# Turning the last gated chunk earlier, and placing two of the merge's sums later, in a decoder layer

## The chip, the cores and the metric

The kernel runs on one core of a Trainium2 chip. The metric is the device time of one execution in microseconds. The times before are 371.0, 371.18 and 372.96 us, median 371.18 us.

## The reference

One decoder layer on 256 tokens of width 1024, all in float32: a pooling mixer and causal attention side by side, a cross-attention into 256 memory tokens, and a SwiGLU feed-forward of inner width 2816. Each of the three parts is added to 2^(1/4) times the residual and normalized. Only the last part matters here:

```
def swiglu(h, w_gate, w_up, w_down):
    return (jax.nn.silu(h @ w_gate) * (h @ w_up)) @ w_down

h = layer_norm(DEEPNORM_ALPHA * h + swiglu(h, w_gate[l], w_up[l], w_down[l]), ln3_g[l], ln3_b[l])
```

## The kernel before

**Precision.** Every product of float32 matrices is made of three fast products: each operand is split into a high half (a cast on ScalarE, `nc.scalar.copy`) and a low half (value minus high half, `nc.vector.tensor_sub` on VectorE), and high x high, high x low and low x high are summed in PSUM. In the profile `w137h` and `w137l` are the halves of weight tile 137, `w132r` a raw weight tile as it was loaded. Weights are loaded and split on the fly (class `Stream`): `ws.get` splits some tiles ahead of use and, where a raw buffer becomes free, issues the next load on SyncE's queue (SP, L122).

**The feed-forward.** The inner width is cut into 11 chunks (`NFC`) of 256 columns. For chunk c the loop (`for c in range(1, NFC)`, L1032) makes the gate and up products in two PSUM banks (`pg`), one per half of the tokens; `gated(c, t, ps)` (L942, L943) applies silu on ScalarE and multiplies on VectorE, giving `sg`. The down products need the gated chunk with its columns on the partitions. So the chunk is turned: `gated_out(c)` transposes its 32x32 blocks on VectorE (L435, `gs`) and writes it to DRAM from SP (L438, `gd`); `gated_in(c)` reads it back with four transfers that put the blocks in their places (L446, `gr`); `gated_split(c)` splits it into `gTh` (L414, ScalarE) and `gTl` (L415, VectorE). For chunks 0 to 9 these steps are spread over the loop's next passes; for chunk 10, the last, they are listed by hand after the loop.

**The down product.** The output has four pieces, upper left C11, upper right C12, lower left C21 and lower right C22: two halves of the tokens by two halves of the columns. The inner chunks 0 to 8 use seven products instead of eight (a Strassen-like scheme): sums of weight blocks and of token blocks go into four shared PSUM banks p1, p5, p6, p7 (`x` in the profile) inside the loop, and the remaining products (`four`, `fourth`) into the accumulators `acc`. Chunks 9 and 10 (`c_dn`, weight tiles 135 to 138) are multiplied plainly, piece by piece, C11, C12, C21, and C22 in two parts of 256 columns (L1150 to L1152). `down()` is a generator that yields after each product. A hand-written table, `events`, says ahead of which of its first 23 steps another piece of work is issued on the other engines.

**The merge.** `merge()` is a second generator, for VectorE. With u1 = p1, u2 = u1 + p6 (L1104) and u3 = u2 + p7 (L1113), it makes r[n] = ALPHA * h + u for the four pieces (`onto`, L1100): r[0] from u1, r[1] from u2 plus p5 (L1110), r[2] from u3, r[3] from u3 plus p5 (L1119). For C12 and C21 r is added into the accumulator, before their products of chunks 9 and 10 (`seed`, L1068): the first of these products overwrites nothing and has to wait for the seed. For C11 r and the finished accumulator are added afterwards (L1174). C22 is seeded (two operations of 256 columns) after its first products (L1157). Statistics (L715), centring and scaling follow piece by piece, and the rows are stored.

**Order.** Each engine works through its own instructions in the order in which the program issues them, and waits for others by semaphores; transfers issued on SP leave in SP's order.

Of the kernel before, what the change touches and what calls it, by code (L numbers as in the profile page):

```python
# [24 lines left out]
NFC = DFF // CW  # L25
# [10 lines left out]
SEVEN, LAG, LATE = 9, 2, 4  # L36
# [6 lines left out]
class Stream:  # L43
# [118 lines left out]
    def next(self):  # L162

        i = len(self.tiles)
        return i + (2 if i < len(self.items) and self.items[i][0] == "sums" else 1)
# [28 lines left out]
def decoder_layer(  # L194
# [21 lines left out]
    def accbank(name):  # L216
        return pa.tile([P, 512], F32, tag="acc", name=name)
# [157 lines left out]
    def proj_n(pss, numbers, yT, last=True):  # L375

        for k in range(KD):
            for t, ps in pss.items():
                three(ps, pair(yT, ALL, k, slice(t * P, (t + 1) * P)), ws.get(numbers, k), k == 0, k == KD - 1)
            if last:  # L380
                ws.done(numbers, k)
            yield
# [22 lines left out]
    def run(gen, n=None):  # L405

        while n is None or n > 0:
            if next(gen, gen) is gen:
                return False
            n = None if n is None else n - 1  # L410
        return True

    def split(h, l, ps):
        nc.scalar.copy(h, ps)  # L414
        nc.vector.tensor_sub(l, ps, r32(h))  # L415
# [14 lines left out]
    def turned(blocks, n, name, queue=nc.sync):  # L430

        st = sp.tile([P, 4, n, 32], F32, name=f"{name}s", tag="pair", bufs=3)
        for at, src in blocks:
            m = src.shape[1]
            nc.vector.transpose(st[:, :, at:at + m, :].rearrange("p j m b -> p m j b"),  # L435
                                src.rearrange("p m (j b) -> p m j b", b=32))
        via = hp.tile([P, 4, n * 32], F32, name=f"{name}d")
        queue.dma_start(via, st.rearrange("p j m b -> p j (m b)"))  # L438
        return via

    def landed(via, n, name, queue=nc.sync, raw=None):

        if raw is None:
            raw = sp.tile([P, 4, n, 32], F32, name=f"{name}r", tag="pair", bufs=3)
        for j in range(4):
            queue.dma_start(raw[32 * j:32 * (j + 1)].rearrange("p i m b -> p i (m b)"),  # L446
                              via[:, j, :].rearrange("(i a) r -> a i r", i=4))
        return raw
# [245 lines left out]
    class Norm:  # L694
# [15 lines left out]
        def measure(self, c0, c1):  # L710
            self.take(self.r[:, c0:c1])
# [55 lines left out]
    def until(gen):  # L767

        for got in gen:
            if got is not None:  # L770
                return got
# [167 lines left out]
    def gated(c, t, ps):  # L939

        sg = sgs[c][:, :, t, :]
        nc.scalar.activation(sg, ps[:, :CW].rearrange("p (f b) -> p f b", f=2), AF.Silu, bias=0.0, scale=1.0)  # L942
        nc.vector.tensor_mul(sg, sg, ps[:, CW:].rearrange("p (f b) -> p f b", f=2))  # L943
# [3 lines left out]
    def gated_out(c):  # L947
        via[c] = turned([(0, sgs[c].rearrange("p f t b -> p (f t) b"))], 4, "g")

    def gated_in(c):  # L950
        via[c] = landed(via[c], 4, "g")
# [3 lines left out]
    def token_sums(c):  # L955
        raw = via[c]
        s_raw[c] = sp.tile([P, 4, 4, 32], F32, name="sraw", tag="pr", bufs=PR_BUFS)
        if c == 0:
            s_raw["fourth"] = nmp.tile([P, KD, P], F32, name="S4", tag="S")
        a11, a21, a12, a22 = [raw[:, :, m, :] for m in range(4)]  # L960
        s1, s2, s3 = [s_raw[c][:, :, m, :] for m in range(3)]
        nc.gpsimd.tensor_add(s1, a21, a22)  # L962
        nc.gpsimd.tensor_sub(s2, s1, a11)  # L963
        nc.gpsimd.tensor_sub(s3, a11, a21)  # L964
        own = s_raw[c][:, :, 3, :]
        s4_raw = own if c == SEVEN - 1 else s_raw["fourth"][:, c].rearrange("p (i b) -> p i b", i=4)
        nc.gpsimd.tensor_sub(s4_raw, a12, s2)

    def token_sums_split(c):
        hl = [sp.tile([P, 4, P], F32R, name=f"S{n}", tag="pr", bufs=PR_BUFS) for n in range(2)]  # L970
        sums_of[c] = [(hl[0][:, m], hl[1][:, m]) for m in range(3)]
        n = 3
        if c == SEVEN - 1:
            s4[c], n = (hl[0][:, 3], hl[1][:, 3]), 4
        split(*[s[:, :n].rearrange("p m (i b) -> p i m b", i=4) for s in hl], s_raw[c][:, :, :n])

    def fourth_split(c0, c1):
        hl = [sp.tile([P, 4, P], F32R, name=f"S4{n}", tag="pr", bufs=PR_BUFS) for n in range(2)]
        for c in range(c0, c1):
            s4[c] = hl[0][:, c - c0], hl[1][:, c - c0]  # L980
        split(*[s[:, :c1 - c0] for s in hl], s_raw["fourth"][:, c0:c1])

    def gated_split(c):
        i, f = divmod(2 * c, KD)
        h, l = [g[:, f:f + 2, :].rearrange("p f (t i b) -> p (f t) i b", t=T, i=4) for g in gT[i]]
        split(h, l, via[c].rearrange("p i m b -> p m i b"))
# [15 lines left out]
    def shared_products(c):  # L1002

        if not shared:
            shared.extend(bank("x") for _ in range(4))
        p1, p5, p6, p7 = shared
        s1, s2, s3 = sums_of[c]
        for numbers, ops in zip(c_sums[c], (((p1, gblock(c, 0, 0), 0), (p6, s2, 512)), ((p5, s1, 0), (p7, s3, 512)))):
            for ps, y, c0 in ops:
                product(ps, y, numbers, c0, c == SEVEN - 1)  # L1010
            ws.done(numbers, 0)
# [14 lines left out]
    def by_row():  # L1026

        for gen in gu1:
            while run(gen, 2):
                yield  # L1030

    for c in range(1, NFC):  # L1032
        sgs.append(sp.tile([P, 2, T, P], F32, name="sg", tag="pr", bufs=PR_BUFS))
        pss = {t: second[t] if c == 1 else accbank("pg") for t in range(T)}
        gu = by_row() if c == 1 else proj_n(pss, c_gu[c], h2T)
        run(gu, 1)
        gated_out(c - 1)
        run(gu, 2)
        if c > 1:
            gated_split(c - 2)  # L1040
            if c - 2 < SEVEN:
                token_sums(c - 2)
        run(gu, 2)
        gated_in(c - 1)
        run(gu, 1)
        if 0 <= c - 2 < SEVEN:
            token_sums_split(c - 2)
        if c == NFC - 1:
            fourth_split(0, 4)
        run(gu)  # L1050
        for t in range(T):
            gated(c, t, pss[t])
        if 0 <= c - LAG < SEVEN:
            shared_products(c - LAG)

# [32 lines left out]
    def merge():  # L1088

        p1, p5, p6, p7 = shared  # L1090
        for t in range(T):
            norms.append(Norm(3, h2[:, t, :]))
        r = [norms[t].r[:, h * 512:(h + 1) * 512] for t in range(T) for h in range(2)]
        tok = [h2[:, t, h * 512:(h + 1) * 512] for t in range(T) for h in range(2)]

        def u(i):
            return sp.tile([P, 512], F32, name=f"u{i}", tag="pr", bufs=PR_BUFS)

        def onto(n, u):
            nc.vector.scalar_tensor_tensor(r[n], tok[n], ALPHA, u, op0=OP.mult, op1=OP.add)  # L1100

        u1, u2 = u(1), u(2)
        nc.scalar.copy(u1, p1)
        nc.vector.tensor_add(u2, u1, p6)  # L1104
        yield
        onto(0, u1)
        yield
        onto(1, u2)
        yield
        nc.vector.tensor_add(r[1], r[1], p5)  # L1110
        yield
        u3 = u(3)
        nc.vector.tensor_add(u3, u2, p7)  # L1113
        yield
        onto(2, u3)
        yield
        onto(3, u3)
        yield
        nc.vector.tensor_add(r[3], r[3], p5)  # L1119
        yield  # L1120

    def down():

# [16 lines left out]
        for piece in (*PIECES[:3], (1, 512, LAST), (1, LAST, D)):  # L1140
# [18 lines left out]
            yield piece  # L1159

    dn, parts = down(), merge()
    events = {
        2: lambda: gated_out(NFC - 1), 4: lambda: fourth_split(4, SEVEN - 1), 6: lambda: gated_split(NFC - 2),
        7: lambda: gated_in(NFC - 1), 18: lambda: gated_split(NFC - 1),
    }
    events.update({step: lambda: run(parts, 1) for step in (8, 9, 11, 13, 14, 16, 17, 19)})
    for step in range(23):
        events.get(step, lambda: None)()
        run(dn, 1)

    until(dn)
    norm = norms[0]
    for c in (0, 256):
        nc.vector.tensor_add(norm.r[:, c:c + 256], norm.r[:, c:c + 256], acc[PIECES[0]][:, c:c + 256])  # L1174
        norm.measure(c, c + 256)

    def measure(norm, ps):
        for c in range(0, ps.shape[1], 256):
# [89 lines left out]
```

## Time and profile before

| | us |
|---|---|
| profiled execution, device time | 370.71 |
| its span, first to last instruction | 368.9 |
| TensorE (PE) busy | 360.5 |
| weight loads of TensorE (PEld) busy | 311.3 |
| VectorE (DVE) busy | 312.1 |
| ScalarE (ACT) busy | 197.3 |
| GpSimd (POOL) busy | 68.9 |
| median of the three runs | 371.18 |

All times are in us from the start of the span. In a row of a timeline stand the start, the duration, the engine, the line, the operation, what it writes and reads, and in brackets the engine's idle time before it with what ended it. Rows of one engine can overlap a little, because an operation starts while the one ahead drains; what an operation costs its queue is the distance to the next start. A matmul's end is modelled, so for TensorE too the starts are what counts.

### The profile page before, as it was taken

Reading aid. Unit: us, or ns where it says so; the run is one execution under the profiler, and the core shown is the slowest. Engines: PE = TensorE matmul, PEld = TensorE weight load, DVE = VectorE, ACT = ScalarE, POOL = GpSimd, SP = SyncE. Lnnn points to the kernel's source line nnn. Section 1 sums busy time; section 2 is a strip of 40 time slices with the busy share of each in tenths; the row PEclk is TensorE's granted clock in tenths of the full one; section 3 lists DMA queues with packets and bytes.
Section 4 is the critical chain, followed back from the end, with each engine's and each line's share of the span. In section 5 each row is a group of like instructions: output and inputs, shape, how many; then the busy total and the mean of one; then the engine's idle time right before and its main releaser. Section 6 shows DMA issues by size and latency. Waiting matters only on the chain.

```text
span 368.9 us, 5709 instructions
## 1 busy us (share of the span) xinstructions
PE 360.5 (98%) x1995; PEld 311.3 (84%) x1995; DVE 312.1 (85%) x462; ACT 197.3 (53%) x298; POOL 68.9 (19%) x102
## 2 busy tenths in 40 slices
PE   9999999999999999999999999999999999999893
PEld 9997998997888899988888888888888888888682
DVE  5778899994699788765879989999998999789974
ACT  5666865753153665564127636754764664579101
POOL 1000058140010003220010024315402422400000
PEclk9999999999999999999999999999999999999998
DMA  7997699699525995944105988779769877656311
GB/s 246 416 421 297 207 318 327 247 253 396 211 89 167 370 372 203 329 148 151 57 2 198 344 287 285 289 245 346 266 224 338 274 270 262 225 170 195 117 49 65
DMA packets 33836, 89.24 MB, mean 242 GB/s; under 512 B 4240, under 2 KB 12304, under 8 KB 33680
## 3 DMA queue, kind: packets, MB, share of 16 engines
q1 hardware_dynamic: 31520, 83.77, 64.0%
q0 software_dynamic: 1712, 4.72, 4.0%
q10 hardware_dynamic: 576, 0.39, 0.3%
q8 instruction: 15, 0.25, 0.3%
q14 instruction: 13, 0.11, 0.1%
HBM read 81.53 MB, written 7.34 MB: 241 GB/s over the span
## 4 chain that ended last, share of the span: by engine, by line
PE 93%; DVE 4%; issue 1%; ACT 0%; DVEq 0%
PE pg L352 11%; PE pg L351 11%; PE pg L353 11%; PE pxk L369 6%; PE pxq L369 6%; PE pqk L487 6%; PE acc L351 4%; PE acc L352 4%; PE acc L353 4%; PE pu L369 3%; PE x L352 2%; PE x L351 2%; PE x L353 2%; PE xv L352 2%; PE xv L351 2%; PE xv L353 2%
## 5 line engine op out<-in xcount | busy, mean ns | idle before, releaser
L962 POOL TENSOR_TENSOR sraw<-gr 128x128 f32<-128x128 f32 x9 | 9.8, 1094 | 94.7 <-DMA gr<-gd 87.8
L724 POOL TENSOR_TENSOR rs<-mv,mhalf 128x1 f32<-128x1 f32 x6 | 4.4, 735 | 100.2 <-DVE mv L722 100.2
L438 POOL DMA_DIRECT2D pd<-ps x4 | 2.4, 612 | 48.4 <-DVE ps L435 48.1
L524 ACT ACTIVATE pr<-pr,mx 128x128 f32<-128x128 f32 (+1 forms) x16 | 7.1, 444 | 8.2 <-DVE mx L555 8.2
L963 POOL TENSOR_TENSOR sraw<-sraw,gr 128x128 f32<-128x128 f32 x9 | 10.7, 1192 | 0.7
L1204 ACT COPY r<-acc 128x512 f32<-128x512 f32 (+1 forms) x2 | 1.0, 480 | 17.2 <-DVE st L715 17.1
L414 ACT CAST h2Th<-tp 128x512 fp32r<-128x512 f32 x4 | 2.4, 588 | 14.6 <-PE tp L425 14.6
L446 POOL DMA_DIRECT2D pt<-pd x16 | 8.8, 555 | 6.6 <-ACT w23h L144 3.7
L942 ACT ACTIVATE sg<-pg 128x256 f32<-128x256 f32 x22 | 7.9, 381 | 3.2 <-PE pg L353 3.1
L964 POOL TENSOR_TENSOR sraw<-gr 128x128 f32<-128x128 f32 x9 | 9.1, 1009 | 0.0
L943 DVE TENSOR_TENSOR sg<-sg,pg 128x256 f32<-128x256 f32 x22 | 8.4, 415 | 0.4 <-ACT sg L942 0.3
L446 POOL DMA_DIRECT2D xr<-xd x12 | 6.6, 560 | 8.5 <-DMA xd<-xs 5.3
L414 ACT CAST gTh<-gr 128x512 fp32r<-128x512 f32 x11 | 6.8, 614 | 2.6 <-DMA gr<-gd 2.6
L415 DVE TENSOR_TENSOR gTl<-gr,gTh 128x512 fp32r<-128x512 f32 x11 | 7.8, 708 | 0.4 <-ACT gTh L414 0.4
L438 POOL DMA_DIRECT2D xd<-xs x3 | 1.7, 576 | 34.0 <-DVE xs L435 34.0
L435 DVE STREAM_TRANSPOSE gs<-sg 128x512 f32<-128x512 f32 x11 | 7.7, 701 | 0.0
L729 DVE SCALAR_TENSOR_TENSOR r<-r,mv,g 128x512 f32<-128x512 f32 (+1 forms) x10 | 7.5, 781 | 0.2
L524 ACT ACTIVATE xpr<-xs,mx 128x256 f32<-128x256 f32 x8 | 3.7, 470 | 7.0 <-DVE mx L535 7.0
L414 ACT CAST S<-sraw 128x384 fp32r<-128x384 f32 (+1 forms) x9 | 4.7, 523 | 4.6 <-POOL sraw L964 4.6
L715 DVE BATCH_NORM_STATS2 st<-r 128x6 f32<-128x512 f32 (+1 forms) x10 | 6.4, 641 | 0.3
L529 DVE RECIPROCAL sm<-sm 128x2 f32<-128x2 f32 x12 | 2.0, 164 | 5.5 <-ACT xpr L524 4.4
L531 DVE TENSOR_SCALAR pr<-pr,sm 128x128 f32<-128x128 f32 (+1 forms) x16 | 6.1, 422 | 0.3
(1389 smaller groups left out, 1501.0 us busy)
## 6 DMA issues: line engine op xcount, KB each, us to landing
gd<-gs SPq DMA_DIRECT2D x11, 256.0 KB, 5.5
gr<-gd SPq DMA_DIRECT2D x44, 64.0 KB, 2.0
pd<-ps POOLq DMA_DIRECT2D x4, 384.0 KB, 4.2
pt<-pd POOLq DMA_DIRECT2D x16, 96.0 KB, 7.3
g<-in_ln_g SPq DMA_DIRECT2D x3, 512.0 KB, 4.4
b<-in_ln_b SPq DMA_DIRECT2D x3, 512.0 KB, 6.1
wr<-in_w_qkv SPq DMA_DIRECT2D x5, 256.0 KB, 4.8
mr<-in_mem_t SPq DMA_DIRECT2D x1, 1024.0 KB, 12.0
```

The costliest lines, as they stand in the source:

```text
L351: nc.tensor.matmul(ps, wa, ya, start=start, stop=False, skip_group_check=part)
L352: nc.tensor.matmul(ps, wa, yb, start=False, stop=False, skip_group_check=part)
L353: nc.tensor.matmul(ps, wb, ya, start=False, stop=stop, skip_group_check=part)
L369: nc.tensor.matmul(pss[f], w[:, s], y, start=k == 0 and f == 0 and n == 0, stop=k == KD - 1 and n == 2, skip_group_check=True)
L414: nc.scalar.copy(h, ps)
L446: queue.dma_start(raw[32 * j:32 * (j + 1)].rearrange("p i m b -> p i (m b)"), via[:, j, :].rearrange("(i a) r -> a i r", i=4))
L487: nc.tensor.matmul(qk[i][:, f, :], w[:, c * P:(c + 1) * P], y, start=k == 0 and f == 0 and w is hi and y is x_hi, stop=k == KD - 1 and w i ...
L524: nc.scalar.activation(dst[:, j, :], src[:, j, :], AF.Exp, bias=mx[:, j:j + 1], scale=sign, accum_out=sm[:, j:j + 1])
L943: nc.vector.tensor_mul(sg, sg, ps[:, CW:].rearrange("p (f b) -> p f b", f=2))
L962: nc.gpsimd.tensor_add(s1, a21, a22)
L963: nc.gpsimd.tensor_sub(s2, s1, a11)
L964: nc.gpsimd.tensor_sub(s3, a11, a21)
```

## The change

Two things move. No operation is added, dropped or resized.

First, the last gated chunk (chunk 10). Its turn and its write to DRAM are issued right behind its gating product inside the loop, instead of at step 2 of the down product; its read back at step 5 instead of 7; its split at step 12 instead of 18.

Second, the merge. Of its sums, onto 0 (upper left) is issued behind the two seeds, when the products of C11 have been issued; onto 3 and its p5 sum (lower right) behind C11's sums and statistics. What stays at the table's steps are u1 and u2 (8), onto 1 (9), its p5 (11), u3 (16) and onto 2 (17).

```diff
@@ the loop over chunks
         for t in range(T):
             gated(c, t, pss[t])
+        if c == NFC - 1:
+            gated_out(c)
         if 0 <= c - LAG < SEVEN:
             shared_products(c - LAG)
@@ merge()
         nc.vector.tensor_add(u2, u1, p6)
-        yield
-        onto(0, u1)
         yield
         onto(1, u2)
         yield
@@
         onto(2, u3)
         yield
+        onto(0, u1)
+        yield
         onto(3, u3)
-        yield
         nc.vector.tensor_add(r[3], r[3], p5)
-        yield
@@ after down()
     events = {
-        2: lambda: gated_out(NFC - 1), 4: lambda: fourth_split(4, SEVEN - 1), 6: lambda: gated_split(NFC - 2),
-        7: lambda: gated_in(NFC - 1), 18: lambda: gated_split(NFC - 1),
+        4: lambda: fourth_split(4, SEVEN - 1), 5: lambda: gated_in(NFC - 1), 6: lambda: gated_split(NFC - 2),
+        12: lambda: gated_split(NFC - 1),
     }
-    events.update({step: lambda: run(parts, 1) for step in (8, 9, 11, 13, 14, 16, 17, 19)})
+    events.update({step: lambda: run(parts, 1) for step in (8, 9, 11, 16, 17)})
     for step in range(23):
         events.get(step, lambda: None)()
         run(dn, 1)

     until(dn)
+    run(parts, 1)
     norm = norms[0]
     for c in (0, 256):
         nc.vector.tensor_add(norm.r[:, c:c + 256], norm.r[:, c:c + 256], acc[PIECES[0]][:, c:c + 256])
         norm.measure(c, c + 256)
+    run(parts)
```

On VectorE, at the end of the chunk loop (`sg` is the gated chunk 10, `gs` its turned blocks, `w127l` and so on the low halves of weight tiles):

```order
 L943 TENSOR_TENSOR sg<-sg,pg 128x2x128 x2
+L435 STREAM_TRANSPOSE gs<-sg 128x4x4x32
 L145 TENSOR_TENSOR w127l<-w124r,w127h 128x1024
 L145 TENSOR_TENSOR w128l<-w125r,w128h 128x1024
 L145 TENSOR_TENSOR w129l<-w126r,w129h 128x1024
 L145 TENSOR_TENSOR w130l<-w127r,w130h 128x1024
-L435 STREAM_TRANSPOSE gs<-sg 128x4x4x32
 L158 TENSOR_TENSOR w131l<-t_2847,w131h 128x1024
```

The turn stands ahead of four weight splits that it stood behind.

On VectorE from the merge to the last p5 sum, before (`u_3603`, `u_3604`, `u_3640` are u1, u2, u3; `gTl` is the low half of chunk 10; the two seeds follow the last row):

```order
L1100 SCALAR_TENSOR_TENSOR r<-h_1881,u_3603 128x512
L158 TENSOR_TENSOR w134l<-t_3106,w134h 128x1024
L1100 SCALAR_TENSOR_TENSOR r<-h_1881,u_3604 128x512
L145 TENSOR_TENSOR w135l<-w130r,w135h 128x1024
L1110 TENSOR_TENSOR r<-r,x 128x512
L145 TENSOR_TENSOR w136l<-w131r,w136h 128x1024
L1113 TENSOR_TENSOR u_3640<-u_3604,x 128x512
L145 TENSOR_TENSOR w137l<-w132r,w137h 128x1024
L1100 SCALAR_TENSOR_TENSOR r<-h_1881,u_3640 128x512 x2
L145 TENSOR_TENSOR w138l<-w133r,w138h 128x1024
L415 TENSOR_TENSOR gTl_2066<-gr,gTh_2065 128x512
L1119 TENSOR_TENSOR r<-r,x 128x512
```

and now (u3 is `u_3651`; line numbers of the changed kernel are 2 higher in `merge` and `seed`, except L1110 and L1113):

```order
L1102 SCALAR_TENSOR_TENSOR r<-h_1881,u_3604 128x512
L158 TENSOR_TENSOR w134l<-t_3106,w134h 128x1024
L1110 TENSOR_TENSOR r<-r,x 128x512
L145 TENSOR_TENSOR w135l<-w130r,w135h 128x1024
L415 TENSOR_TENSOR gTl_2066<-gr,gTh_2065 128x512
L145 TENSOR_TENSOR w136l<-w131r,w136h 128x1024
L145 TENSOR_TENSOR w137l<-w132r,w137h 128x1024
L1113 TENSOR_TENSOR u_3651<-u_3604,x 128x512
L1102 SCALAR_TENSOR_TENSOR r<-h_1881,u_3651 128x512
L145 TENSOR_TENSOR w138l<-w133r,w138h 128x1024
L1070 TENSOR_TENSOR acc<-r,acc 128x512 x2
L1102 SCALAR_TENSOR_TENSOR r<-h_1881,u_3603 128x512
```

Chunk 10's low half stands ahead of w136l instead of behind w138l, and between u2's sum (just ahead of both pieces) and the seeds three sums fewer are left. On ScalarE the cast to `gTh` moves in the same way, from behind the cast of w138h to ahead of that of w136h. On SP:

```order
 L446 DMA gr<-gd 32x4x128 x4
+L438 DMA gd<-gs 128x512
 L122 DMA w131r<-in_w_down 128x1024
 L122 DMA w132r<-in_w_down 128x1024
 L122 DMA w133r<-in_w_down 128x1024
-L438 DMA gd<-gs 128x512
 L446 DMA gr<-gd 32x4x128 x4
```

The write of the turned chunk leaves ahead of three weight loads; its read back (last row) stands behind them as before. TensorE's order is the same in both kernels.

## The prediction

> **What bounds the kernel now.** I read the page first (busy shares), then the list of waits of TensorE, then the table by stretches around the one wait that matters, and then the timelines of TensorE, VectorE and ScalarE there. PE is TensorE, DVE is VectorE, ACT is ScalarE.
>
> ```profile
> span 368.9 us, 5709 instructions
> ...
> PE 360.5 (98%) x1995; PEld 311.3 (84%) x1995; DVE 312.1 (85%) x462; ACT 197.3 (53%) x298; POOL 68.9 (19%) x102
> ```
>
> PE is busy for all but 8 us, so only PE's waits and the short tail behind its last product can be won. The two longest waits of PE over the whole span (total, times, longest):
>
> ```profile
> PE acc L1152 <- DVE gTl L415: 1.8, 1, 1.8
> PE out L1213 <- ACT diag L1211: 1.5, 1, 1.5
> ```
>
> The first is the target: a down product (L1152) waits for gTl, the low half of the last gated chunk (chunk 10), which DVE writes in L415. The other lies at the very end. In the table by stretches (PE, PEld, DVE, ACT, POOL busy, clock, DMA share, GB/s) the stretch of the wait stands out:
>
> ```profile
> 338.00:347.30 9.30, 9.30 (x43) 7.66 (x41) 9.30 (x12) 4.44 (x5) 0.00 (x0) 1.00 0.46 141
> 347.30:353.50 6.20, 4.41 (x19) 3.05 (x18) 5.52 (x11) 0.00 (x0) 0.00 (x0) 1.00 0.00 0
> ```
>
> Before it DVE has not one idle moment (9.30 of 9.30) while ACT is half idle: up to the wait DVE's queue sets the time, and what stands in that queue ahead of gTl is what PE waits for. PE's timeline (start, duration, idle before):
>
> ```profile
> 347.25 0.39 PE L1151 MATMUL acc<-w137l,gTh 128*128 128x512 f32 x1
> 349.41 0.50 PE L1152 MATMUL acc<-w137h,gTl 128*128 128x512 f32 x1 [1.77 <-DVE gTl L415]
> ...
> 350.21 0.39 PE L1152 MATMUL acc<-w138h,gTl 128*128 128x512 f32 x1
> 350.61 0.50 PE L1150 MATMUL acc<-w135h,gTh 128*128 128x512 f32 x1
> ...
> 353.48 0.40 PE L1157 MATMUL acc<-w135h,gTh 128*128 128x256 f32 x2
> ...
> 356.46 0.39 PE L1150 MATMUL acc<-w135h,gTh 128*128 128x512 f32 x1
> ...
> 358.95 0.39 PE L1152 MATMUL acc<-w138h,gTl 128*128 128x512 f32 x1
> ```
>
> Undisturbed, products of this size start every (358.95 - 356.46) / 11 = 0.226 us. From 347.25 to 353.48 there are 17 starts, 17 x 0.226 = 3.85; it took 6.23. So the wait, a smaller one at 350.61 (for the seed of C12, below) and the slower steps behind both cost 2.38 us. That is what can be won here.
>
> **The change part by part.** DVE's rows around it:
>
> ```profile
> 327.92 0.42 DVE L943 TENSOR_TENSOR sg<-sg,pg 128x256 f32<-128x256 f32 x1 [0.26 <-ACT sg L942]
> 328.85 1.23 DVE L145 TENSOR_TENSOR w127l<-w124r,w127h 128x1024 fp32r<-128x1024 f32 x1 [0.52 <-ACT w127h L144]
> ...
> 331.31 1.22 DVE L145 TENSOR_TENSOR w129l<-w126r,w129h 128x1024 fp32r<-128x1024 f32 x1
> ...
> 333.59 0.70 DVE L435 STREAM_TRANSPOSE gs<-sg 128x512 f32<-128x512 f32 x1
> 334.22 1.18 DVE L158 TENSOR_TENSOR w131l<-t,w131h 128x1024 fp32r<-128x1024 f32 x1
> ...
> 339.39 0.68 DVE L1100 SCALAR_TENSOR_TENSOR r<-h,u 128x512 f32<-128x512 f32 x1
> 339.99 1.22 DVE L158 TENSOR_TENSOR w134l<-t,w134h 128x1024 fp32r<-128x1024 f32 x1
> ...
> 347.54 1.22 DVE L145 TENSOR_TENSOR w138l<-w133r,w138h 128x1024 fp32r<-128x1024 f32 x1
> 348.67 0.68 DVE L415 TENSOR_TENSOR gTl<-gr,gTh 128x512 fp32r<-128x512 f32 x1
> 349.27 0.68 DVE L1119 TENSOR_TENSOR r<-r,x 128x512 f32<-128x512 f32 x1
> 349.87 1.28 DVE L1068 TENSOR_TENSOR acc<-r,acc 128x512 f32<-128x512 f32 x2
> ```
>
> In this queue an operation costs its distance to the next start: 0.63 for the turn (333.59 to 334.22), 0.60 for a sum of 512 columns (339.39 to 339.99, 349.27 to 349.87).
>
> *The turn (L435)* moves from 333.59 to behind the gating product, 328.3. Its 0.63 lie in an idle gap: DVE waited 0.52 for w127h and stands still again before w129l, whose high half comes late from ACT:
>
> ```profile
> 330.22 1.06 ACT L144 CAST w129h<-w126r 128x1024 fp32r<-128x1024 f32 x1 [0.26 <-PE x L353]
> ...
> 337.73 0.39 PE L352 MATMUL acc<-w127l,gTh 128*128 128x512 f32 x1
> ```
>
> That cast waits for PE and ends at 331.28, so w129l starts at 331.31 as before; w127l and w128l are 0.08 later, and PE first reads w127l at 337.73. Cost 0, and 0.63 less in the queue behind. If that cover were gone, it would be 0.54 (0.63 less the 0.09 between w128l's end, about 331.22, and 331.31).
>
> *The transfer.* SP issues the write of the turned chunk at about 329.05 instead of 334.32, ahead of three weight loads that wait for w127l to w129l and so cannot leave before 330.1 (the end of w127l); they follow 0 to 0.1 later, and the read back stands behind them. In the old place the trip was (SP's queue, then the landing times of the write and of one read, min/median/max):
>
> ```profile
> 334.32 0.33 SPq L438 DMA_DIRECT2D gd<-gs  x1
> 338.61 1.75 SPq L446 DMA_DIRECT2D gr<-gd  x4
> ...
> DMA to landing us min/median/max: 3.3/4.2/5.5
> ...
> DMA to landing us min/median/max: 1.8/2.0/3.4
> ```
>
> So the chunk is back at 329.05 + 4.3 + 1.75 + 2.0 = 337.1, or with the longest of each at 339.7.
>
> *The split.* The cast to gTh (0.52 on ACT) now follows w135h and stands ahead of w136h, w137h and w138h:
>
> ```profile
> 337.70 1.06 ACT L144 CAST w135h<-w130r 128x1024 fp32r<-128x1024 f32 x1
> ...
> 341.78 1.06 ACT L144 CAST w138h<-w133r 128x1024 fp32r<-128x1024 f32 x1 [0.30 <-PE acc L353]
> ```
>
> It may start at 338.76; ACT is half idle in this stretch and its later casts are held by PE, so it costs nothing if the chunk is back. What DVE wants of it follows from the start of the seeds, worked out below (347.70): backwards from there stand w138l (1.13, from 347.54 to 348.67), u3 and onto 2 (0.73 and 0.60), w137l and w136l (1.13 each), so w136l starts at 342.98. The chunk may therefore land as late as 342.98 - 0.52 - 1.06 = 341.4: 1.7 us behind the longest trip. gTl itself stands ahead of w136l, at about 342.4, and PE asks for it 0.226 behind 347.25. That wait is gone by more than 4 us.
>
> *What PE waits for next.* The seed of C12 (L1068, 349.87): PE starts C12 at 350.61, 0.74 behind its start. In the new order the turn (0.63), onto 0 (0.60), onto 3 (0.60) and the last p5 sum (0.60) no longer stand ahead of it, and gTl still does: 349.87 - 2.43 = 347.44. Against that, two sums now directly follow the one whose result they read (u2 then onto 1, u3 then onto 2; before, another operation stood between). What that costs shows in the weight sums, where each reads the one ahead:
>
> ```profile
> 311.34 0.69 DVE L95 TENSOR_TENSOR w120r<-w120r,w119r 128x512 f32<-128x512 f32 x1
> 312.07 0.69 DVE L96 TENSOR_TENSOR w120r<-w120r 128x512 f32<-128x512 f32 x1
> ```
>
> 0.73 from start to start instead of 0.60, so 2 x 0.13: the seed starts at 347.70 and PE may start C12 at 348.44. Undisturbed PE would get there at 347.25 + 5 x 0.226 = 348.38: it waits 0.06. w138l starts at 346.57, ends at 347.79 and is read at 347.93: 0.14 in hand. Bounds of this term: with no penalty the seed is 0.2 ahead of PE (all 2.4 won); with the penalty on twice as many sums PE waits 0.3 more. I take the row: 2.38 - 0.06 = 2.3 won.
>
> The Trainium skill (VectorE: DVE Perf Modes, The DRAIN you can't avoid) holds that a chain of copies takes as long with a semaphore behind each as with one at the end, "the semaphore costs nothing extra here"; by that the penalty would be 0 and the gain 2.4. The 0.73 against 0.60 of the rows differ from it for operations that read the one ahead, so I go by the rows.
>
> *The tail.* onto 0 now stands behind the seeds, onto 3 and its p5 sum behind the statistics of C11:
>
> ```profile
> 353.80 0.76 DVE L1068 TENSOR_TENSOR acc<-r,acc 128x256 f32<-128x256 f32 x2 [0.88 <-PE acc L1157]
> ...
> 359.38 0.43 DVE L715 BATCH_NORM_STATS2 st<-acc 128x6 f32<-128x256 f32 x1 [0.94 <-PE acc L1152]
> ...
> 360.69 0.43 DVE L715 BATCH_NORM_STATS2 st<-acc 128x6 f32<-128x256 f32 x1 [0.35 <-PE acc L1152]
> 362.01 0.43 DVE L715 BATCH_NORM_STATS2 st<-acc 128x6 f32<-128x256 f32 x1 [0.89 <-PE acc L1152]
> ```
>
> In the old order the seeds, the C11 sums and their statistics took from 349.87 to 352.92, where the idle 0.88 begins: 3.05. In the new one the three moved sums come in between, each next to one that reads its result or is read by it: 3 x 0.73 = 2.19. 347.70 + 3.05 + 2.19 = 352.94 for the last two seeds; PE reads these only behind C21, so they are hidden. From them to the first statistic of C21 DVE works 4.64 (353.80 to 358.44, where the idle 0.94 begins): 357.6, while C21 is there at 359.38 - 2.3 = 357.1. DVE is 0.5 late where it had 0.94 in hand; the idle 0.35 and 0.89 ahead of the next two statistics absorb that, with 0.7 left at the last one. Cost 0; without that cover, 1:1. The loads of the last norm's weights stand behind the read back on SP, before as after, and leave no later.
>
> **Sum.** 370.71 us (profiled execution: span 368.9 and 1.8 around it) - 2.3 = 368.4. The median of the runs shown is 371.18, 0.47 above that execution, so 371.18 - 2.3 = 368.9, which I predict.
>
> **The rivals.**
>
> *A cover that isn't there.* If the turn is not hidden (w129l later by 0.54) or the penalty falls on more sums, the seed of C12 comes 0.5 to 0.6 later and PE waits for it: 2.3 - 0.6 = 1.7 won, 369.5. For it: w138l and the seed have 0.14 and -0.06 in hand, so every delay of DVE counts 1:1. Against: the cast of w129h hangs on PE, which doesn't change.
>
> *The wait moves to the tail.* DVE has next to no idle time from 331 to 357.6 in the new order. Should the sums behind C11 take much longer than in the rows, the last statistics start late and the gain is eaten there: 2.3 + 0.7 = 3.0 us of delay give 371.2. For it: the slack sinks from 2.2 (0.94 + 0.35 + 0.89) to 0.7. Against: all these durations stand in rows.
>
> *The chunk comes back late, and ACT holds everything behind it: slower.* The cast of gTh now blocks w136h to w138h, and with them w136l to w138l and the seeds. Each us beyond 341.4 costs 1 us. To end slower than before it must land after 343.7, a trip of 14.7 us from the issue of the write. For it: the write and the reads now share the queue with three 512 KB loads. If it takes 17 us (landing at 346), 4.6 late: 371.18 - 2.3 + 4.6 = 373.5. Against: the longest write (5.5) and read (3.4) that the trace shows, with 1.75 of issue, make 10.7.
>
> *The change doesn't do what it says.* The turn could not start at 328.3 if its buffer were still taken. It is the one of the read back of chunk 8, whose last readers are these:
>
> ```profile
> 317.98 1.44 POOL L967 TENSOR_TENSOR sraw<-gr,sraw 128x128 f32<-128x128 f32 x1
> ...
> 321.61 0.69 DVE L415 TENSOR_TENSOR gTl<-gr,gTh 128x512 fp32r<-128x512 f32 x1
> ```
>
> Both are done by 322.3, so this is all but excluded; the time would be 371.2.
>
> **How the numbers follow.** Forecast 0.78; cover gone 0.08 (369.5); tail or no effect 0.08 (371.2); late chunk 0.06 (373.5). 0.5%, or 1.86 us here, is about what a measurement of this kernel can tell from no change: faster means below 369.3. The forecast's own range is 368.4 (by the profiled execution) to 369.3; I leave 0.04 of it to the middle: faster 0.74, same 0.20, slower 0.06. The range reaches 0.5 below the forecast's own lower end for the spread of the runs (371.0 to 371.18 for two of them, 370.71 for the profiled one), and up past the first rival: 367.9 to 370.5.
>
> **What the profile of the changed kernel would show.** Right: the turn at 328.3 and w129l still at 331.31; the read back issued at 333 to 334; the cast of gTh at 338.8 with no idle time put down to a DMA; no wait of PE for gTl, at most 0.1 for the seed of C12; the two dependent pairs at 0.73; the last product 2.3 us earlier; the first statistic of C21 with no idle before it and the last one still waiting for PE. Wrong: ACT idle before gTh, PE waiting for w138l or the seed by 0.5 or more, or the last statistic released by DVE itself. A gain under 1.86 would make the forecast wrong.

## The result, and the profile after

The changed kernel takes 369.59 us (median of six, 368.9 to 370.04); the kernel before, run beside it, 371.42 (371.0 to 372.96). The ratio is 0.9943, with a 95% interval of 0.9921 to 0.9964: 2.1 us less, between 1.3 and 2.9. The profiled execution took 369.38. Its page:

```profile
span 367.6 us, 5709 instructions
...
PE 360.9 (98%) x1995; PEld 312.0 (85%) x1995; DVE 311.6 (85%) x462; ACT 197.0 (54%) x298; POOL 64.9 (18%) x102
```

The same instructions, nearly the same busy times, a shorter span. TensorE's longest wait now (total, times, longest):

```profile
PE out L1215 <- ACT diag L1213: 1.5, 1, 1.5
```

The wait of 1.8 us for gTl is gone from the list; what leads it is the one at the very end, which was there before. TensorE's timeline of the place (start, duration), and then its weight loads (PEld):

```profile
346.48 0.39 PE L1150 MATMUL acc<-w135h,gTh 128*128 128x512 f32 x1
...
348.29 0.39 PE L1152 MATMUL acc<-w137h,gTl 128*128 128x512 f32 x1
348.51 0.39 PE L1150 MATMUL acc<-w138h,gTh 128*128 128x512 f32 x1
348.74 0.44 PE L1151 MATMUL acc<-w138l,gTh 128*128 128x512 f32 x1
349.02 0.40 PE L1152 MATMUL acc<-w138h,gTl 128*128 128x512 f32 x1
349.29 0.51 PE L1150 MATMUL acc<-w135h,gTh 128*128 128x512 f32 x1
349.63 0.40 PE L1151 MATMUL acc<-w135l,gTh 128*128 128x512 f32 x1
...
352.15 0.40 PE L1157 MATMUL acc<-w135h,gTh 128*128 128x256 f32 x2
...
348.29 0.19 PEld L1150 LDWEIGHTS acc<-w138h,gTh 128*128 128x128 f32 x1
348.68 0.19 PEld L1151 LDWEIGHTS acc<-w138l,gTh 128*128 128x128 f32 x1 [0.20 <-DVE w138l L145]
...
349.28 0.19 PEld L1150 LDWEIGHTS acc<-w135h,gTh 128*128 128x128 f32 x1 [0.31 <-DVE acc L1070]
349.39 0.19 PEld L1151 LDWEIGHTS acc<-w135l,gTh 128*128 128x128 f32 x1
```

For all kernels one measure serves from here on, called **the stretch**: from the start of C11's first product (346.48) to that of C22's first products (L1157, 352.15). It spans 24 starts, so 24 x 0.2265 = 5.43 us undisturbed. It took 7.82 before (345.66 to 353.48) and takes 5.67 now: 2.15 won. From the L1157 products to the start of the last down product it is 8.21 us in both kernels, so nothing is given back behind it.

What is left of the loss, 5.67 - 5.43 = 0.24, shows in the weight loads. Undisturbed, a load starts one step ahead of its product: that of w138h at 348.29, its product at 348.51. The load of w138l was due at 348.51 and starts at 348.68, because VectorE is done with w138l only at 347.41 + 1.22 = 348.63; the load for C12's first product waits for the seed and starts with its product (349.28 and 349.29) instead of a step ahead. The next load then follows 0.11 behind, and its product comes 0.34 after C12's first one instead of 0.227. Such a slow step follows most stops here: in the kernel before, the next product starts 0.33 behind the one that waited for gTl.

The two profiled executions differ by only 1.33. The rest, 0.82, is a later start of the stretch in the execution after (346.48 against 345.66), with the same work on TensorE ahead of it. TensorE is 0.81 late already at 157 us, long before the first instruction that the change moves, the turn at 329, and the kernels below reach the stretch at anything from 345.55 to 347.23: this is variation between executions and not the change. Times of day in the prediction are to be read 0.82 later in the execution after.

VectorE's rows that answer to those shown before:

```profile
329.19 0.71 DVE L435 STREAM_TRANSPOSE gs<-sg 128x512 f32<-128x512 f32 x1
...
332.12 1.23 DVE L145 TENSOR_TENSOR w129l<-w126r,w129h 128x1024 fp32r<-128x1024 f32 x1
...
339.01 0.68 DVE L1106 TENSOR_TENSOR u<-u,x 128x512 f32<-128x512 f32 x1
339.73 0.69 DVE L1102 SCALAR_TENSOR_TENSOR r<-h,u 128x512 f32<-128x512 f32 x1
...
343.21 0.69 DVE L415 TENSOR_TENSOR gTl<-gr,gTh 128x512 fp32r<-128x512 f32 x1
...
347.41 1.22 DVE L145 TENSOR_TENSOR w138l<-w133r,w138h 128x1024 fp32r<-128x1024 f32 x1
348.54 1.29 DVE L1070 TENSOR_TENSOR acc<-r,acc 128x512 f32<-128x512 f32 x2
...
360.68 0.43 DVE L715 BATCH_NORM_STATS2 st<-acc 128x6 f32<-128x256 f32 x1 [0.89 <-PE acc L1152]
```

VectorE starts on gTl 5.1 us before TensorE's first product with it (343.21 against 348.29). The seeds start at 348.54, and TensorE starts C12 at 349.29, 0.75 behind, as before the change (0.74). The last statistic still waits 0.89 us for TensorE. What did not look as expected is the transfer. ScalarE's casts, the write and the reads on SP, and then the landing times of the write and of one read (min/median/max):

```profile
338.51 1.06 ACT L144 CAST w135h<-w130r 128x1024 fp32r<-128x1024 f32 x1
341.06 0.62 ACT L414 CAST gTh<-gr 128x512 fp32r<-128x512 f32 x1 [1.49 <-DMA gr<-gd]
...
329.93 0.34 SPq L438 DMA_DIRECT2D gd<-gs  x1
334.75 1.80 SPq L446 DMA_DIRECT2D gr<-gd  x4
...
DMA to landing us min/median/max: 2.0/2.0/2.0
...
DMA to landing us min/median/max: 4.8/5.2/5.4
```

The write lands sooner than before (2.0 us; 4.2 for this chunk then), the reads much later (4.8 to 5.4 us behind their issue; 1.8 to 2.0 for this chunk then). ScalarE stands still 1.49 us until they have landed.

### The profile page after: what moved, and what is told of

The parts are those of the page before. It is cut to its first block, busy times and chain, and to the rows that moved or that the text cites. A ratio compares the mean times of both kernels' runs of the same rounds, so it can differ in the third digit from the quotient of the medians.

```text
span 367.6 us, 5709 instructions
## 1 busy us (share of the span) xinstructions
PE 360.9 (98%) x1995; PEld 312.0 (85%) x1995; DVE 311.6 (85%) x462; ACT 197.0 (54%) x298; POOL 64.9 (18%) x102
## 4 chain that ended last, share of the span: by engine, by line
PE 83%; issue 11%; DVE 2%; DMA 2%; POOL 1%; ACT 0%; DVEq 0%; POOLq 0%; ACTq 0%
PE pg L353 11%; PE pg L351 11%; PE pg L352 11%; PE pxk L369 6%; PE pqk L487 6%; PE acc L351 5%; PE acc L352 5%; PE acc L353 5%; PE pu L369 3%; PE x L353 2%; PE x L351 2%; PE x L352 2%; DMA xd<-xs 2%; PE busy L458 1%; PE pv L351 1%
## 5 line engine op out<-in xcount | busy, mean ns | idle before, releaser
L962 POOL TENSOR_TENSOR sraw<-gr 128x128 f32<-128x128 f32 x9 | 6.8, 751 | 98.7 <-DMA gr<-gd 68.1
L963 POOL TENSOR_TENSOR sraw<-sraw,gr 128x128 f32<-128x128 f32 x9 | 9.3, 1037 | 0.7
L964 POOL TENSOR_TENSOR sraw<-gr 128x128 f32<-128x128 f32 x9 | 7.5, 838 | 0.0
L967 POOL TENSOR_TENSOR S<-gr,sraw 128x128 f32<-128x128 f32 x8 | 6.6, 831 | 0.0
```

## The experiments

The theory: the gain is that of VectorE's queue, which sets when gTl, w138l and the seed of C12 are there; TensorE waits for the latest of them, and each delay of VectorE counts 1:1 once it is late. The rivals: one of the two parts alone does all of it; the early turn is a risk because the chunk's trip holds ScalarE; the tail eats part of it.

All kernels, with the stretch (from one profiled execution each; the gain is against 7.82) and the ratio to the kernel before. The intervals of most of the faster ones overlap, so it is the stretch that tells these apart:

| kernel | stretch | gain in the stretch | ratio, 95% interval |
|---|---|---|---|
| before | 7.82 | | 1 |
| chunk moved, merge as before | 7.22 | 0.60 | 0.9976 (0.9959 to 0.9993) |
| merge changed, chunk as before | 6.55 | 1.27 | 0.9959 (0.9945 to 0.9972) |
| the change, but the turn late | 6.27 | 1.55 | 0.9958 (0.9944 to 0.9972) |
| the change | 5.67 | 2.15 | 0.9943 (0.9921 to 0.9964) |
| the change, and three sums more behind C11 | 5.68 | 2.14, less 1.06 in the tail | 0.9959 (0.9937 to 0.9981) |
| the change, sums apart | 5.46 | 2.36 | profiled execution only |
| the change, seed of C12 first | 5.44 | 2.38 | 0.9936 (0.9913 to 0.9959) |
| the change, read back ahead of the loads | 5.67 | 2.15 | profiled execution only |
| the change, read back very late | 11.08 | -3.26 | 1.0068 (1.0046 to 1.009) |

### The merge alone

The changed kernel with the chunk's steps as before:

```diff
-        if c == NFC - 1:
-            gated_out(c)
@@ events
-        4: lambda: fourth_split(4, SEVEN - 1), 5: lambda: gated_in(NFC - 1), 6: lambda: gated_split(NFC - 2),
-        12: lambda: gated_split(NFC - 1),
+        2: lambda: gated_out(NFC - 1), 4: lambda: fourth_split(4, SEVEN - 1), 6: lambda: gated_split(NFC - 2),
+        7: lambda: gated_in(NFC - 1), 18: lambda: gated_split(NFC - 1),
```

> Only the merge's sums stand later (onto 0 behind the seeds, onto 3 and its p5 sum behind C11's statistics); the chunk is turned, read and split in its old places. The measure is the stretch of TensorE from the first product of weight tile 135 for C11 to the first product of C22 (L1157): 7.82 us before, 5.67 with the whole change, 24 x 0.2265 = 5.43 undisturbed. My theory (VectorE's in-order queue sets when PE goes on, 1:1): gTl starts two sums earlier, less two penalties for reading the operation ahead: 348.67 - 1.20 + 0.26 = 347.73 on the clock of the profile before; PE wants it at 347.48 and has it 0.74 behind its start, 348.47: a wait of 1.0 for gTl, none for the seed, and 0.2 of slow steps behind it. Stretch 6.7, 1.1 won, 370.3 us. Rival (the sums are the whole gain, the chunk's move only follows): 2.1 won, 369.3.

TensorE's and VectorE's timelines of this kernel:

```profile
348.34 0.50 PE L1150 MATMUL acc<-w137h,gTl 128*128 128x512 f32 x1 [0.82 <-DVE gTl L415]
...
347.60 0.68 DVE L415 TENSOR_TENSOR gTl<-gr,gTh 128x512 fp32r<-128x512 f32 x1
348.20 1.28 DVE L1068 TENSOR_TENSOR acc<-r,acc 128x512 f32<-128x512 f32 x2
```

The wait for gTl shrinks from 1.77 to 0.82 and that for the seed vanishes: the three sums alone, two of them taken out from ahead of gTl and the third from ahead of the seeds, are worth 1.27 of the 2.15. The theory, with 1.1 won, came near; that the sums are the whole gain is excluded.

### The chunk alone

The kernel before, with the turn, the read back and the split moved:

```diff
+        if c == NFC - 1:
+            gated_out(c)
@@ events
-        2: lambda: gated_out(NFC - 1), 4: lambda: fourth_split(4, SEVEN - 1), 6: lambda: gated_split(NFC - 2),
-        7: lambda: gated_in(NFC - 1), 18: lambda: gated_split(NFC - 1),
+        4: lambda: fourth_split(4, SEVEN - 1), 5: lambda: gated_in(NFC - 1), 6: lambda: gated_split(NFC - 2),
+        12: lambda: gated_split(NFC - 1),
```

> Only the last chunk is turned, read and split sooner; the merge's sums stand in their old places. My theory: the wait for gTl is gone, and the queue behind it is shorter by the turn alone (0.63): w138l starts at 347.51, ends at 348.73, where PE wants it at 347.93 (0.86 late), and the seed of C12 starts at 349.24, so PE begins C12 at 349.98 instead of 348.38: in all 1.6 late and some 0.2 of slow steps. Stretch 7.2, 0.5 to 0.6 won, 370.9 us. The waits named will be w138l and the seed, not gTl. Rival (gTl was the wait, so its early split is the whole gain): 2.1 won, 369.3, and no wait for w138l.

TensorE's timeline of this kernel:

```profile
349.42 0.50 PE L1153 MATMUL acc<-w138l,gTh 128*128 128x512 f32 x1 [0.73 <-DVE w138l L145]
...
350.62 0.50 PE L1152 MATMUL acc<-w135h,gTh 128*128 128x512 f32 x1 [0.47 <-DVE acc L1070]
```

gTl is early, and the wait moves on to what now stands last in VectorE's queue: 0.73 for w138l and 0.47 for the seed, as the theory had it (7.2). The two parts alone win 1.27 + 0.60 = 1.87, less than the 2.15 of both, since TensorE waits for the later of two things and one part alone leaves the other late.

### The turn late

The changed kernel with the turn back at step 2; read back and split stay early:

```diff
-        if c == NFC - 1:
-            gated_out(c)
@@ events
-        4: lambda: fourth_split(4, SEVEN - 1), 5: lambda: gated_in(NFC - 1), 6: lambda: gated_split(NFC - 2),
+        2: lambda: gated_out(NFC - 1), 4: lambda: fourth_split(4, SEVEN - 1), 5: lambda: gated_in(NFC - 1), 6: lambda: gated_split(NFC - 2),
```

> The whole change but for the turn, which stays in its old place on VectorE and so does its write on SP; the split stays early. It makes the chunk come back late with the cast to gTh standing ahead of those of w136h to w138h on ScalarE. On the clock of before: write issued 334.3, reads 338.6 to 340.4, landed 342.4 to 343.8 (reads of 2.0 to 3.4) or 345.6 (5.2, as measured with the change). My theory (ScalarE is held, everything behind it moves 1:1): w136h is ready 1.58 behind the landing, 344.0 to 347.2, where VectorE wants it at 343.6; the seed of C12 comes at 348.7 to 351.9 and PE begins C12 0.7 later. Between 1.0 won and 2.0 lost, 370.4 to 373.4 us, with ScalarE idle 4 to 7 us ahead of the cast to gTh. Rival (the hold on ScalarE is hidden): only the 0.63 of the turn is lost, the seed starts at 348.33, 1.5 won, 369.9.

ScalarE's and VectorE's timelines of this kernel, and TensorE's one wait:

```profile
342.81 0.62 ACT L414 CAST gTh<-gr 128x512 fp32r<-128x512 f32 x1 [3.03 <-DMA gr<-gd]
...
349.34 1.29 DVE L1068 TENSOR_TENSOR acc<-r,acc 128x512 f32<-128x512 f32 x2
...
349.48 0.50 PE L1149 MATMUL acc<-w138l,gTh 128*128 128x512 f32 x1 [0.37 <-DVE w138l L145]
```

The seed stands 349.34 - 346.68 = 2.66 behind the start of the stretch, against 348.54 - 346.48 = 2.06 in the changed kernel: 0.60 later, and the stretch is 0.60 longer. That is the 0.63 that the turn costs VectorE's queue, no more, although ScalarE stood still for 3.03 us. The theory (370.4 to 373.4) missed, and the rival came in. By the clock of before the chunk was there at 342.81 - 1.02 = 341.79, sooner than the 342.4 that was given. The last moment is 341.4 + 0.6 = 342.0, as the turn makes VectorE 0.6 later anyway, so this kernel does not reach the point from which the wait costs. So the early turn is worth its place in VectorE's idle gap, which is the figure of the prediction's first rival (0.54 to 0.63), and the later chunk by itself cost nothing yet.

### The read back ahead of the loads

The changed kernel with the read back issued right behind the write, so that SP's queue has the three weight loads behind it:

```diff
         if c == NFC - 1:
             gated_out(c)
+            gated_in(c)
@@ events
-        4: lambda: fourth_split(4, SEVEN - 1), 5: lambda: gated_in(NFC - 1), 6: lambda: gated_split(NFC - 2),
+        4: lambda: fourth_split(4, SEVEN - 1), 6: lambda: gated_split(NFC - 2),
```

> The whole change, and the four reads of the last chunk stand on SP right behind its write, ahead of the three weight loads instead of behind them. With the change the reads took 4.8 to 5.4 us to land, the cast to gTh waited 1.5 for them and had 1.1 to spare. My theory (the reads are slow because they queue behind the bytes of the three loads): the reads leave at about 332, 2.1 behind the write's issue, take 2 us each and are in by 336; ScalarE no longer waits for a DMA ahead of gTh; the weight loads leave 2 to 3 later and are still in time; the stretch stays at 5.67, the time within 0.2 us of the change. Rival (the loads' delay reaches w136h to w138h): ScalarE waits for w131r to w133r there, and the stretch grows by what it waits beyond 1.1.

SP's queue, the landing time of one read, and the cast:

```profile
332.73 2.36 SPq L446 DMA_DIRECT2D gr<-gd  x4
335.18 0.46 SPq L122 DMA_DIRECT2D w131r<-in_w_down  x1
...
DMA to landing us min/median/max: 2.2/2.4/3.1
...
340.23 0.61 ACT L414 CAST gTh<-gr 128x512 fp32r<-128x512 f32 x1
```

Ahead of the loads a read lands in 2.2 to 3.1 us instead of 4.8 to 5.4, and the cast waits for no transfer. That is what made the trip long: 64 KB reads behind three loads of 512 KB each that were still under way. The stretch is 5.67 all the same, as in the changed kernel: the 1.49 us for which ScalarE stood still there were covered. The one execution took 370.13 us, 0.54 above the median of the changed kernel and not within the 0.2 that was expected; against the profiled execution of that kernel it is 0.75 more, and it reaches the stretch 0.75 later.

### The read back very late

To reach the point from which ScalarE's standing still costs, a small transfer that must wait for the upper right sum (r[1] with its p5) is put ahead of the read back on SP:

```diff
+    def late_read():
+        held = hp.tile([P, 32], F32, name="held", bufs=1)
+        nc.sync.dma_start(held, norms[0].r[:, 512:544])
+        gated_in(NFC - 1)
+        gated_split(NFC - 1)
@@ events
-        4: lambda: fourth_split(4, SEVEN - 1), 5: lambda: gated_in(NFC - 1), 6: lambda: gated_split(NFC - 2),
-        12: lambda: gated_split(NFC - 1),
+        4: lambda: fourth_split(4, SEVEN - 1), 6: lambda: gated_split(NFC - 2),
+        12: late_read,
```

> The whole change, but the read of the last chunk is held on SP behind a small transfer (32 columns of r[1] to DRAM, used by nothing) that waits for VectorE's p5 sum of C12. It makes the chunk late while the cast to gTh stands ahead of those of w136h to w138h: the slower rival of the prediction. On the clock of before: p5 done at 341.3, reads issued 341.8 to 343.5, landed 345.5 or somewhat later behind the small transfer. My theory (ScalarE's in-order queue is held, VectorE and PE behind it 1:1 beyond a landing of 341.4): 4 us late, stretch 9.7 to 10.3, 373.5 us, slower than before, with PE waiting for w136l or gTh. Rival (the hold is hidden, since nothing of gTh is needed before PE reads it at 347): stretch 5.67 to 6.5, 369.6 to 370.5.

The cast, the seeds, TensorE's waits, and then the table by stretches (PE, PEld, DVE, ACT, POOL busy, clock, DMA share, GB/s):

```profile
345.71 0.62 ACT L414 CAST gTh<-gr 128x512 fp32r<-128x512 f32 x1 [6.61 <-DMA gr<-gd]
...
352.05 1.29 DVE L1070 TENSOR_TENSOR acc<-r,acc 128x512 f32<-128x512 f32 x2
...
PE acc L1151 <- DVE w138l L145: 1.5, 1, 1.5
PE acc L1151 <- DVE w136l L145: 0.8, 1, 0.8
...
346.00:349.50 3.50, 2.26 (x8) 1.05 (x6) 2.88 (x3) 3.18 (x4) 0.00 (x0) 1.00 0.73 235
349.50:352.20 2.70, 1.03 (x5) 0.50 (x4) 2.67 (x5) 0.00 (x0) 0.00 (x0) 1.00 0.00 2
352.20:355.60 3.40, 3.40 (x8) 2.65 (x9) 3.19 (x8) 0.00 (x0) 0.00 (x0) 0.52 0.00 0
```

This execution reaches the stretch 0.35 later than the one before (346.01 against 345.66), so the chunk landed at 345.71 - 0.35 = 345.36 by the prediction's clock: 3.96 behind the 341.4 that it named as the last moment. The seeds stand 352.05 - 346.01 = 6.04 behind the start of the stretch, 3.98 later than in the changed kernel. At the price of the prediction's slower rival, 1 us for 1 us, its threshold fits to 0.02 us. The stretch grew by more, 11.08 - 5.67 = 5.41. The other 1.4 are in the third row: for 3.4 us TensorE's granted clock is 0.52, and products there start 0.43 us apart instead of 0.227. That row comes behind two in which TensorE was busy for 2.26 + 1.03 = 3.29 of 6.20 us, with four waits between 0.17 and 1.50 us. The single wait of 1.77 us in the profiled execution of the kernel before left the clock at 1.00.

Neither need hold for every execution. A time of 3.4 us at 0.52 lowers the mean clock by some 3.4 x 0.48 / 371 = 0.004, an estimate. Of the ten executions of this kernel five have a mean granted clock of 0.995 to 0.997, and their median is 373.7 us, near the 373.5 that was expected; the other five, at 0.987 to 0.992, took 374.3 to 375.9. Of the nineteen of the kernel before that were run beside it, four have 0.991 or 0.992 and took 373.1 to 373.5, the others 0.995 to 0.998 and 371.0 to 372.4. So the wait of 1.77 us may have been enough in those four; where the clock was low in them no trace shows.

By the Trainium skill (TensorE: Matmul & The Clock Gate, Part 1: The HAM clock gate) half clock follows an idle window of some 3.4 us. The length of the slow time agrees. No idle time here is that long: in this execution shorter waits close together, 2.9 us of 6.2, went ahead of the low clock.

### The sums apart

The changed kernel with an operation between u2 and onto 1, and between u3 and onto 2, so that no sum follows the one whose result it reads:

```diff
-    events.update({step: lambda: run(parts, 1) for step in (8, 9, 11, 16, 17)})
+    events.update({step: lambda: run(parts, 1) for step in (8, 11, 13, 14, 17)})
```

> The whole change, with u2 and onto 1, and u3 and onto 2 no longer next to each other on VectorE (a weight split stands between); the same operations, each with the same semaphores. My theory (an operation that reads the result of the one right ahead starts 0.12 to 0.13 later): u2 and u3 cost 0.60 instead of 0.72, the seed of C12 comes 0.25 earlier on the clock of the stretch (2.06 behind the stretch's start with the change, 1.8 here), PE has neither wait left, the stretch is 5.43 to 5.5 instead of 5.67. Rival (the Trainium skill's rule that a semaphore behind each operation costs nothing): 0.72 for both places or 0.60 for both, the seed where it was, 5.67.

VectorE's timeline of this kernel:

```profile
339.64 0.68 DVE L1106 TENSOR_TENSOR u<-u,x 128x512 f32<-128x512 f32 x1
340.24 1.22 DVE L158 TENSOR_TENSOR w134l<-t,w134h 128x1024 fp32r<-128x1024 f32 x1
...
348.92 1.29 DVE L1070 TENSOR_TENSOR acc<-r,acc 128x512 f32<-128x512 f32 x2
```

From u2's sum to the next start it is 0.60, against 0.72 in the changed kernel (339.01 to 339.73). The seeds stand 348.92 - 347.10 = 1.82 behind the start of the stretch instead of 2.06: 0.24 sooner, which is the 2 x 0.12 of the two pairs. TensorE waits for nothing in the stretch, and it takes 5.46. (The one execution took 369.79 us, 0.41 more than the profiled one of the changed kernel: it reaches the stretch 0.62 later and gains 0.21 in it.) The Trainium skill (VectorE: DVE Perf Modes, The DRAIN you can't avoid) finds no cost for a semaphore behind each operation of a chain of copies; a pair of which the second reads the first costs 0.12 us more here, and the two pairs take these 0.24 from the seed.

### The seed of C12 first

The changed kernel with u3 and onto 2, which C12 doesn't need, behind the seed of C12:

```diff
-    events.update({step: lambda: run(parts, 1) for step in (8, 9, 11, 16, 17)})
+    events.update({step: lambda: run(parts, 1) for step in (8, 9, 11)})
@@ down()
         seed(*PIECES[1], acc[PIECES[1]])
+        run(parts, 2)
         seed(*PIECES[2], acc[PIECES[2]])
```

> The whole change, and u3 and onto 2 (which only C21 needs) stand behind the seed of C12 instead of ahead of it. The stretch is 5.67 with the change and 5.43 undisturbed. My theory (the 0.24 left is a wait of 0.05 to 0.1 for w138l and the seed plus slow steps that such a wait brings): the seed and w138l come 1.33 earlier, PE has no wait left, the stretch is 5.43 to 5.45, 0.2 won beyond the change, 369.2 us, and the last statistic still waits for PE. Rival (the slow steps come with the first products into C12, whatever was waited for): the step of 0.34 at C12's start stays and the stretch is 5.55 to 5.6.

VectorE's seed, TensorE at the start of C12 and at the end of the stretch, and the last statistic:

```profile
346.92 0.69 DVE L1070 TENSOR_TENSOR acc<-r,acc 128x512 f32<-128x512 f32 x1
...
348.90 0.39 PE L1151 MATMUL acc<-w135h,gTh 128*128 128x512 f32 x1
349.13 0.39 PE L1152 MATMUL acc<-w135l,gTh 128*128 128x512 f32 x1
...
351.62 0.40 PE L1158 MATMUL acc<-w135h,gTh 128*128 128x256 f32 x2
360.15 0.43 DVE L715 BATCH_NORM_STATS2 st<-acc 128x6 f32<-128x256 f32 x1 [0.68 <-PE acc L1153]
```

The seed starts 2 us before C12; TensorE's steps are all 0.227 and the stretch is 5.44, which is all there is to win (7.82 - 5.43 = 2.39). The step at the start of C12, 0.34 in the changed kernel (349.29 to 349.63), is 0.23 here: the slow steps go with the waits. The sums that went behind the seed don't show in the tail, where the last statistic still waits 0.68 for TensorE. This is the fastest of the kernels by its median, 369.26, but against the change itself (0.9936 and 0.9943) the intervals lie over each other; that it is faster by 0.23 us is the profile's word alone.

### Three sums more behind C11

The changed kernel with onto 3, which writes the same values each time, issued four times:

```diff
-        onto(3, u3)
+        for _ in range(4):
+            onto(3, u3)
```

> The whole change, with onto 3 done four times instead of once (the same result), so that VectorE works 1.8 to 2.2 longer behind C11's statistics. With the change the last statistic still waits 0.89 for PE. My theory (the tail's cover is that 0.89 and no more; beyond it 1:1): the first statistic of C21 starts 1.8 to 2.2 later, the last one is released by VectorE itself, 0.9 to 1.3 later than with the change, 370.5 to 370.9 us; the stretch stays at 5.67. Rival (VectorE's tail is hidden behind PE's last products of C22 or the stores): 369.6.

VectorE's timeline of this kernel, with TensorE's last down product:

```profile
351.60 2.86 DVE L1102 SCALAR_TENSOR_TENSOR r<-h,u 128x512 f32<-128x512 f32 x4
...
359.65 0.28 PE L1153 MATMUL acc<-w138h,gTl 128*128 128x256 f32 x1
359.85 0.42 DVE L715 BATCH_NORM_STATS2 st<-acc 128x6 f32<-128x256 f32 x1
...
361.49 0.26 DVE L722 BATCH_NORM_AGGREGATE mv<-st 128x2 f32<-128x24 f32 x1
```

Three sums of 0.72 put VectorE 2.16 later. None of the four statistics waits for TensorE any more, and they are aggregated 361.49 - 359.65 = 1.84 behind the start of the last down product, where the changed kernel does it at 0.78: 1.06 late. Of the 2.16 the waits ahead of the statistics took 1.1, and the rest went into the end. The changed kernel's tail thus has about 1 us in hand, and the prediction's second rival begins beyond it.

## Why the prediction was right, point by point

It said 368.9 us, 367.9 to 370.5, faster; measured were 369.59 and faster. The mechanism and nearly every moment of it held. (Moments below are the prediction's, plus 0.82.)

- **The turn** was to be hidden ahead of w129l (332.13). It was: w129l starts at 332.12. The kernel with the late turn shows that this cover is worth 0.60.
- **The wait for gTl** is gone. VectorE starts on gTl at 343.21 (343.2 was given); as TensorE went on 0.74 behind that start before, 4.3 us are in hand (more than 4 were given).
- **The seed of C12** was to start at 348.52 and C12 at 349.26. They start at 348.54 and 349.29. The two pairs cost 0.12 each (0.13 was taken).
- **The tail** was to cost nothing, with 0.7 in hand at the last statistic; it has 0.89, and three sums more show that the slack is real and ends near 1.1.
- **What was mis-sized is the term "I take the row: 2.38 - 0.06 = 2.3 won".** The stretch kept 0.24 and 2.15 were won. Two steps of its working failed. The first is that w138l is "read at 347.93: 0.14 in hand": that is the start of its product, but the weight load comes a step of 0.227 sooner, and w138l was 0.12 too late for it (348.63 against 348.51). The second is that the sum counted only how late the seed is, and not the slow step behind such a stop. Measured are 0.28 and 0.27 where TensorE waits for w138l and for the seed, and then 0.34 from C12's first product to the next, instead of 0.227 (the other 21 steps make up the remaining 0.03). The 2.38 held such steps and they were taken to go wholly. Where neither wait is left (sums apart, seed first) they do.
- **The transfer was told wrong in both halves, and it didn't matter.** "The longest write (5.5) and read (3.4)" were taken for a bound of 10.7 from the issue of the write (with 1.75 of issue); it took 341.06 - 329.93 = 11.1. The step that failed is that rows of reads behind nothing were used for reads behind three loads. The prediction's mark for wrong, "ACT idle before gTh", did occur. It cost nothing, because the chunk had until 341.4 + 0.82 = 342.2; this threshold, worked out backwards from the seed, fits the very late read back. With some 3.5 us more the rival would have been the outcome.
- **The result itself** stands 0.7 above the forecast. By the medians 1.83 are won (371.42 - 369.59), just under the 1.86 that the prediction set for itself; by the ratio 2.1, just over. The ratio goes with the means (371.72 and 369.59), and two long executions of the kernel before, 372.36 and 372.96, raise the first. So whether 1.86 was reached is not decided. "The last product 2.3 us earlier" came out as 2.15 on the clock of the stretch. The mis-sized term is 0.15 of the 0.7, and 0.24 is that the kernel before came out at 371.42 rather than 371.18; what is left, 0.3, is less than the interval tells apart.

## What to carry to other kernels

Where one engine's queue is full and another waits for several of its results, work out the moment of each result and of each demand, not only of the one that is waited for now: the gain ends at the next result that is late, here first w138l, then the seed. Of a moved transfer, price the queue that it then stands in, and work out backwards how late it may land; that margin, and not the landing time, decides. For a weight the demand is the start of its load, one step ahead of the product. And count the slow step behind a stop: here two stops of 0.04 to 0.05 us cost 0.24 together.

## What the runs showed of the hardware

- A chain of short waits can be enough for the clock: in the profiled execution of the very late read back four of 0.2 to 1.5 us within 6.2 us, TensorE busy 3.29 of them, were followed by 3.4 us at a granted clock of 0.52. By their mean clock, half of its executions show no sign of this. One wait of 1.77 us left the clock at 1.00 in the one execution of the kernel before that was traced.
- A weight load starts a step of 0.227 us ahead of its product. Where TensorE waited for an operand of C12's first product, load and product start together (349.28 and 349.29), and the next product starts 0.34 us later.
- Reads of 64 KB that stood on one queue behind three loads of 512 KB took 4.8 to 5.4 us to land, and 2.2 to 3.1 ahead of them. The write of 256 KB took 2.0 us where it was issued ahead of the loads, and 4.0 to 4.3 behind them (kernel before, merge alone, turn late).
- Two VectorE operations of 512 columns start 0.72 us apart where the second reads the first's result, and 0.60 where it doesn't.
